# A hybrid encoder layer on one core: operand stores on another queue, and a norm's last blocks moved among the next products

## The chip, the core and the metric

The kernel runs on one core of one Trainium2 chip. TensorE (PE) multiplies, with its weight loads (PEld) beside it; VectorE (DVE), ScalarE (ACT) and GpSimd (POOL) compute; SyncE (SP), ACT and POOL issue DMAs, each from a queue that is worked off in order. The time is device microseconds of one execution; the median of the runs counts.

## What is computed

One encoder layer over 2048 frames of width 1024, in float32. Cut to what matters here:

```
mix = concat([y_pool, y_ssm]) @ w_out
h = layer_norm(alpha * h + mix, g1, b1)
f = (silu(h @ w1) * (h @ w3)) @ w2        # w1, w3: 1024 x 2816, w2: 2816 x 1024
r = alpha * h + f
h = layer_norm(r + sigmoid(r @ w_gate) * (p @ w_ple), g2, b2)
```

with alpha = 2 ** 0.25. Everything up to `mix` (input projection, pooling, state space, GLU) and the last line are untouched by the change.

## The kernel before

**Products.** Each float32 operand is split into a high and a low part (`split`, L100 to 102: a cast on ACT, a subtraction on VectorE), and each product is three matmuls (`mm3`, L122 to 125). In the gated unit the 2048 frames stand as two halves h of 1024, and each multiplication of 2 x 2 blocks is done with seven products in place of eight. `pieces7` (L826) forms the seven operands: its `put` (L834) splits one into a tile `xo` (tag `xb`, two buffers in `xbp`, L1249) and stores it, 512 KB, to DRAM (L837): `Gv` for the pieces of g = silu(.) * (.), 154 stores, `Xv` for pieces of h, 28, `Wv` for pieces of the gate's weights, 28. All 210 go out on POOL's queue. They come back as `gv` (L996, POOL), `xv` and `gw`.

**Stages around the change.** `out_proj` adds the mix to `pre`; `out_ln(h, q)` (L712) normalises 512 frames: statistics of four blocks on VectorE, a power on POOL (L739), the normalisation on ACT (L718), 32 transposes on TensorE into `zb` (L722), copies into `ze` (L724) and stores to DRAM `Hd` on ACT's queue (L725). `load_h` (L858) loads 128 columns of `Hd` on POOL's queue, multiplies by g1 and adds b1 (L861, VectorE), and stores the result to `Hn` (L862, 16 stores of 512 KB on POOL's queue). `xprep0` and `xprep0_rest` make the pieces `xv` of half 0 from it, `xprep1` those of half 1, which `put` stores. `w13(h)` then runs 11 pairs of columns with 2 x 7 products of twelve matmuls each into banks `fb`; ACT and VectorE form g from the banks (L943 to L970), and `pieces7` of g runs beside the next pair's products. `w2_half(h)` multiplies by w2: `gv` pieces against weight pieces into banks `f`; the first result for a tile `HR` is an ACT copy (L1025), later ones are added by VectorE (L1026); once a tile is full, `hl` is loaded from `Hn` on SP's queue (L1015) and VectorE adds ALPHA * hl (L1016). The HR tiles share the memory of the g tiles (`slp`, tag `sl`), so the third one waits until the last g has been read by the sixth piece's split, put(5). Weights `wq` come on SP's queue (L774, three buffers), five products ahead (LEAD); sums of them (`ws`) and the pieces `wv` are made by ACT and VectorE, the sums in tiles `x` (five buffers), of which `pre` takes four.

**Order.** A scheduler orders each engine's instructions from a simulated timeline; the order of the program's text and the rates given to `drive` (steps of the second generator for each step of the first) shape it. Around the change the program's text is:

```
for _ in range(2):
    more()                                  # weights, one product each
drive(out_ln(1, 1), xprep0_rest(), 0.5)
for _ in range(2, LEAD):
    more()
drive(w13(0), xprep1(), 0.5)
drive(w2_half(0), None, 0)
```

Of the kernel before, what the change touches and what calls it, by code (L numbers as in the profile page):

```python
# [12 lines left out]
F32 = mybir.dt.float32  # L13
# [27 lines left out]
def trunk_kernel(  # L41
# [120 lines left out]
    Td = drp.tile([128, NG, 128], F32, name="Td")  # L162
    Rd = drp.tile([NC, 16, 2, 240], F32, name="Rd")
    Gd = drp.tile([128, NG, 128], F32, name="Gd")
    Hn = drp.tile([2, 8, 128, 2, 512], F32, name="Hn")
    Xv = drp.tile([7, 4, 128, 1024], F32, name="Xv")
    Gv = drp.tile([2, NF // 2, 7, 128, 1024], F32, name="Gv")
    Wv = drp.tile([7, 4, 128, 1024], F32, name="Wv")
# [540 lines left out]
            for t in range(4):  # L709
                V.scalar_tensor_tensor(pre[t][:, ns], pre[t][:, ns], ALPHA, acc[t], MUL, ADD)  # L710

    def out_ln(h, q):  # L712
        pre = blk[h, q][3]
        for t in range(4):
            mv, rstd = ln_stats([pre[t][:, 0:512], pre[t][:, 512:1024]])
            nb = sm.tile([128, 1], F32, tag="nb", name="nb")
            V.scalar_tensor_tensor(nb, mv[:, 0:1], -1.0, rstd, MUL, MUL)
            A.activation(pre[t], pre[t], AF.Identity, bias=nb, scale=rstd)  # L718
            for m2 in range(2):
                b = tbank([128, 4, 128], "zb")  # L720
                for m in range(4):
                    PE.transpose(b[:, m], pre[t][:, 512 * m2 + 128 * m:512 * m2 + 128 * m + 128], ident)  # L722
                e = evp.tile([128, 4, 128], F32, tag="ev", name="ze")
                A.copy(e, b)  # L724
                A.dma_start(Hd[512 * m2:512 * m2 + 512, h, 4 * q + t].rearrange("(m p) j -> p m j", p=128), e)  # L725
            yield
# [86 lines left out]
    def all_weights():  # L813
        for h in range(2):
            for pi in range(NF // 2):
                for w in (w1, w3):
                    yield from weights7(w[2 * pi], w[2 * pi + 1], 1)
            for gi, pairs in W2:
                np_ = len(pairs)
                for mu in range(np_):  # L820
                    yield from weights7(w2[4 * gi + mu], w2[4 * gi + np_ + mu], np_, sums_b if gi else sums_x)
        for n in range(len(PAIRS)):
            yield from rows7(n)
# [5 lines left out]
    def pieces7(b11, b12, b21, b22, dst):  # L829

        tt = xp.tile([128, 2, 512], F32, tag="x", name="tt")
        t1, t2 = tt[:, 0], tt[:, 1]

        def put(i, src):  # L834
            v = operand(xbp, "xb", "xo")
            split(v[:, 0], v[:, 1], src)
            G.dma_start(dst[i], v.bitcast(F32).rearrange("p a n -> p (a n)"))  # L837

        put(0, b11)
        yield  # L840
# [12 lines left out]
        put(5, b22)
        yield
        put(6, t2)
        yield

    def load_h(h, k, pool, tag):  # L858
        t = pool.tile([128, 2, 512], F32, tag=tag, name="hl")
        G.dma_start(t, Hd[128 * k:128 * k + 128, h].rearrange("p (q t) j -> p q (t j)", q=2))  # L860
        V.tensor_scalar(t, t, g1[:, k:k + 1], b1[:, k:k + 1], MUL, ADD)  # L861
        G.dma_start(Hn[h, k], t)  # L862
        return t

    X = [[[None] * 4 for _ in range(7)] for _ in range(2)]
# [114 lines left out]
    def w2_half(h):  # L980
# [19 lines left out]
        for gi, pairs in W2:  # L1000
# [3 lines left out]
            for mu in range(np_):  # L1004
                if gi == 0:
                    t = slp.tile([128, 2, 2, 512], F32, tag="sl", name="HR")
                    hr[2 * mu], hr[2 * mu + 4] = t[:, 0], t[:, 1]
                    for m in (2 * mu + 1, 2 * mu + 5):
                        hr[m] = operand32("HR", mu)
                else:  # L1010
                    um = per_units[gi] + mu
                    if um < 8:
                        hl = xp.tile([128, 2, 512], F32, tag="x", name="hl")
                        with tc.issue_after(latest[0].ins):
                            SP.dma_start(hl, Hn[h, um])  # L1015
                        V.scalar_tensor_tensor(hr[um], hl, ALPHA, hr[um], MUL, ADD)  # L1016
                done_w = []
                for m0 in range(0, per, 2):
                    ms = [per * mu + m0, per * mu + m0 + 1]
# [229 lines left out]
    xbp = mid_pools.enter_context(tc.tile_pool(name="xbp", bufs=2, reuse_waits="tile"))  # L1249
    wqp = mid_pools.enter_context(tc.tile_pool(name="wqp", bufs=3, reuse_waits="tile"))  # L1250
    stream[0] = all_weights()
    for _ in range(2):
        more()
    drive(out_ln(1, 1), xprep0_rest(), 0.5)
    for _ in range(2, LEAD):
        more()
    drive(w13(0), xprep1(), 0.5)
    drive(w2_half(0), None, 0)
    xload1(latest[0])
    drive(w13(1), wprep(), 0.5)  # L1260
# [79 lines left out]
```

## Time and profile before

| | |
|---|---|
| timed runs | 2088.03, 2088.08, 2091.39 us, median 2088.08 |
| the profiled execution | 2085.38 us, of which the span is 2083.6 |
| mean granted clock of TensorE | 0.986 |
| busy: TensorE, VectorE, ACT, POOL | 2008.1, 1611.5, 876.8, 337.0 us |
| mean DMA rate | 218 GB/s |

The rows are of the profiled execution. PEclk is the clock granted to TensorE, as a share of full speed. In a timeline row the bracket holds the idle time of that engine before the instruction and what ended it, as inferred from semaphores; a matmul's length includes what overlaps the next one.

### The profile page before, as it was taken

To read this page: it belongs to the slowest core of one execution; us is meant where nothing else is said; L and a number is where in the kernel's file an instruction comes from. 1 tells how busy PE (TensorE), PEld (TensorE's weight loads), DVE (VectorE), ACT (ScalarE), POOL (GpSimd) and SP (SyncE) were. 2 spreads that over 40 slices of the span, in tenths; PEclk is the share of its full clock that TensorE was granted. 3 is DMA by queue.
4 is the path that set the end of the run, shared out by engine and by line. 5 is a ranking of instruction groups with operands and counts; after the bars stand their busy time and mean duration, and the time that the engine had idled before them with its cause. 6 is when DMAs were issued, how large, how long until landed. Compare 5 with 4: busy or idle time off the path is not lost.

```text
span 2083.6 us, 25684 instructions
## 1 busy us (share of the span) xinstructions
PE 2008.1 (96%) x8968; PEld 1626.0 (78%) x8968; DVE 1611.5 (77%) x2886; ACT 876.8 (42%) x1515; POOL 337.0 (16%) x595
## 2 busy tenths in 40 slices
PE   8999899999899999999899999999999799999996
PEld 6877778787688878888688888888888688878885
DVE  7599699658678887676698878887776588878885
ACT  3543546645544554444322245555444322233342
POOL 2002101211112111103122111111012221211111
PEclk9999999999999999999999999999999999999998
DMA  7636757657646754439777775665346986782221
GB/s 248 221 109 227 263 181 233 232 192 263 211 188 247 257 209 159 165 122 373 302 290 295 289 245 222 236 229 197 127 151 211 390 314 255 283 288 91 92 71 46
DMA packets 161041, 454.45 MB, mean 218 GB/s; under 512 B 15424, under 2 KB 51616, under 8 KB 160912
## 3 DMA queue, kind: packets, MB, share of 16 engines
q0 software_dynamic: 73632, 265.10, 34.1%
q1 hardware_dynamic: 53296, 156.26, 21.6%
q10 hardware_dynamic: 33984, 31.46, 4.4%
q8 instruction: 70, 1.15, 0.2%
q14 instruction: 59, 0.48, 0.1%
HBM read 291.83 MB, written 163.02 MB: 218 GB/s over the span
## 4 chain that ended last, share of the span: by engine, by line
PE 54%; issue 20%; DMA 12%; DVE 7%; POOL 4%; ACT 3%; POOLq 0%; SPq 0%; ACTq 0%; DVEq 0%
PE f L123 6%; PE f L124 6%; PE f L125 6%; PE fb L123 6%; PE fb L125 5%; PE fb L124 5%; PE ab L123 2%; PE ab L124 2%; PE ab L125 2%; DMA Gv<-xo 2%; PE ib L125 2%; PE ib L123 2%; PE ib L124 2%; POOL Gv L837 2%; DMA hl<-Hd 2%
## 5 line engine op out<-in xcount | busy, mean ns | idle before, releaser
L123 PE MATMUL fb<-xv,wv 128*128 128x512 f32 x1232 | 482.9, 396 | 6.6 <-ACT u L967 4.8
L124 PE MATMUL fb<-xv,wv 128*128 128x512 f32 x1232 | 485.6, 394 | 0.0
L125 PE MATMUL fb<-xv,wv 128*128 128x512 f32 x1232 | 479.9, 395 | 0.2 <-DVE wv L102 0.2
L101 ACT CAST wv<-ws 128x512 fp32r<-128x512 f32 x296 | 183.3, 620 | 384.1 <-PE f L125 170.5
L123 PEld LDWEIGHTS fb<-xv,wv 128*128 128x128 f32 x1232 | 232.4, 189 | 62.0 <-ACT u L967 7.1
L125 PEld LDWEIGHTS fb<-xv,wv 128*128 128x128 f32 x1232 | 232.1, 188 | 54.1 <-DVE wv L102 0.7
L124 PEld LDWEIGHTS fb<-xv,wv 128*128 128x128 f32 x1232 | 232.4, 189 | 53.5
L123 PE MATMUL f<-gv,wv 128*128 128x512 f32 x616 | 242.7, 397 | 19.6 <-ACT HR L1025 17.1
L102 DVE TENSOR_TENSOR wv<-ws,wv 128x512 fp32r<-128x512 f32 x296 | 202.9, 686 | 68.3 <-ACT wv L101 67.9
L124 PE MATMUL f<-gv,wv 128*128 128x512 f32 x616 | 243.9, 396 | 0.0
L1026 DVE TENSOR_TENSOR HR<-HR,f 128x512 f32<-128x512 f32 x304 | 201.1, 682 | 45.7 <-PE f L125 42.2
L125 PE MATMUL f<-gv,wv 128*128 128x512 f32 x616 | 234.3, 396 | 0.0
L837 POOL DMA_DIRECT2D Gv<-xo x154 | 82.2, 534 | 562.7 <-DVE xo L102 549.2
L101 ACT CAST wv<-wq 128x512 fp32r<-128x512 f32 x198 | 122.7, 621 | 96.7 <-PE f L125 73.0
L123 PEld LDWEIGHTS f<-gv,wv 128*128 128x128 f32 x616 | 116.9, 190 | 49.1 <-ACT HR L1025 18.4
L102 DVE TENSOR_TENSOR wv<-wq,wv 128x512 fp32r<-128x512 f32 x198 | 135.4, 685 | 20.2 <-ACT wv L101 19.7
L125 PEld LDWEIGHTS f<-gv,wv 128*128 128x128 f32 x616 | 116.8, 190 | 26.7
L124 PEld LDWEIGHTS f<-gv,wv 128*128 128x128 f32 x616 | 116.8, 190 | 26.3
L101 ACT CAST xo<-tt 128x512 fp32r<-128x512 f32 x120 | 74.6, 621 | 120.1 <-DMA Gv<-xo 49.2
L996 POOL DMA_DIRECT2D gv<-Gv x154 | 81.6, 530 | 228.1 <-PE f L125 181.0
L102 DVE TENSOR_TENSOR xo<-tt,xo 128x512 fp32r<-128x512 f32 x120 | 82.3, 686 | 40.1 <-ACT xo L101 39.5
L123 PE MATMUL ob<-wh,mx 128*128 128x512 f32 x256 | 102.3, 409 | 7.4 <-ACT sg L681 7.4
(317 smaller groups left out, 3551.8 us busy)
## 6 DMA issues: line engine op xcount, KB each, us to landing
Gv<-xo POOLq DMA_DIRECT2D x154, 512.0 KB, 3.2
gv<-Gv POOLq DMA_DIRECT2D x154, 512.0 KB, 7.6
wq<-in_w_dram SPq DMA_DIRECT2D x132, 512.0 KB, 4.3
wr<-in_w_out_dram SPq DMA_DIRECT2D x32, 512.0 KB, 4.7
Xv<-xo POOLq DMA_DIRECT2D x28, 512.0 KB, 3.8
xv<-Xv POOLq DMA_DIRECT2D x28, 512.0 KB, 5.8
Wv<-xo POOLq DMA_DIRECT2D x28, 512.0 KB, 3.3
gw<-Wv POOLq DMA_DIRECT2D x28, 512.0 KB, 5.8
```

What stands on the lines that cost most here:

```text
L101: A.copy(hi, src)
L102: V.tensor_tensor(lo, src, hi.bitcast(F32), SUB)
L123: PE.matmul(ps, ah, bh, start=first, stop=False, **kw)
L124: PE.matmul(ps, ah, bl, start=False, stop=False, **kw)
L125: PE.matmul(ps, al, bh, start=False, stop=last, **kw)
L837: G.dma_start(dst[i], v.bitcast(F32).rearrange("p a n -> p (a n)"))
L996: G.dma_start(v.bitcast(F32).rearrange("p a n -> p (a n)"), Gv[h, pi, i])
L1026: return V.tensor_tensor(o, o, bank, ADD)
```

## The change

1. `put` stores on SP's queue (all 210 stores).
2. `Hn` and its 16 stores are gone. `w2_half` loads `hl` from `Hd`, the normalised values before g1 and b1; VectorE multiplies by alpha * g1, a scalar per partition, in place of alpha, and alpha * b1 comes in as the bias of an ACT activation that takes the place of the copy into HR. Both vectors are made once, by two small VectorE instructions.
3. `out_ln(1, 1)` no longer runs before `w13(0)` but beside it, chained ahead of `xprep1()`, at one step for two products; its `ze` tiles come from another pool, and the sums of the first w1 weights lie in an `xb` tile, since `pre` still holds four of the `x` tiles.

```
@@ -141,6 +141,9 @@
     glub = column("glub", glu_b, 4)
     g1 = column("g1", ln1_g, 8)
     b1 = column("b1", ln1_b, 8)
+    gb1a = cst.tile([128, 2, 8], F32, name="gb1a")
+    V.tensor_scalar(gb1a[:, 0], g1, ALPHA, None, MUL)
+    V.tensor_scalar(gb1a[:, 1], b1, ALPHA, None, MUL)
     poolw = cta.tile([128, 4, 128], F32, name="poolw")
     G.dma_start(poolw, pool_w[0].rearrange("g c d -> c g d"))
 
@@ -162,7 +165,6 @@
     Td = drp.tile([128, NG, 128], F32, name="Td")
     Rd = drp.tile([NC, 16, 2, 240], F32, name="Rd")
     Gd = drp.tile([128, NG, 128], F32, name="Gd")
-    Hn = drp.tile([2, 8, 128, 2, 512], F32, name="Hn")
     Xv = drp.tile([7, 4, 128, 1024], F32, name="Xv")
     Gv = drp.tile([2, NF // 2, 7, 128, 1024], F32, name="Gv")
     Wv = drp.tile([7, 4, 128, 1024], F32, name="Wv")
@@ -709,7 +711,7 @@
             for t in range(4):
                 V.scalar_tensor_tensor(pre[t][:, ns], pre[t][:, ns], ALPHA, acc[t], MUL, ADD)
 
-    def out_ln(h, q):
+    def out_ln(h, q, room=None):
         pre = blk[h, q][3]
         for t in range(4):
             mv, rstd = ln_stats([pre[t][:, 0:512], pre[t][:, 512:1024]])
@@ -720,7 +722,7 @@
                 b = tbank([128, 4, 128], "zb")
                 for m in range(4):
                     PE.transpose(b[:, m], pre[t][:, 512 * m2 + 128 * m:512 * m2 + 128 * m + 128], ident)
-                e = evp.tile([128, 4, 128], F32, tag="ev", name="ze")
+                e = evp.tile([128, 4, 128], F32, tag="ev", name="ze") if room is None else room([128, 4, 128], "ze")
                 A.copy(e, b)
                 A.dma_start(Hd[512 * m2:512 * m2 + 512, h, 4 * q + t].rearrange("(m p) j -> p m j", p=128), e)
             yield
@@ -814,7 +816,7 @@
         for h in range(2):
             for pi in range(NF // 2):
                 for w in (w1, w3):
-                    yield from weights7(w[2 * pi], w[2 * pi + 1], 1)
+                    yield from weights7(w[2 * pi], w[2 * pi + 1], 1, sums_b if h + pi == 0 and w is w1 else sums_x)
             for gi, pairs in W2:
                 np_ = len(pairs)
                 for mu in range(np_):
@@ -834,7 +836,7 @@
         def put(i, src):
             v = operand(xbp, "xb", "xo")
             split(v[:, 0], v[:, 1], src)
-            G.dma_start(dst[i], v.bitcast(F32).rearrange("p a n -> p (a n)"))
+            SP.dma_start(dst[i], v.bitcast(F32).rearrange("p a n -> p (a n)"))
 
         put(0, b11)
         yield
@@ -859,7 +861,6 @@
         t = pool.tile([128, 2, 512], F32, tag=tag, name="hl")
         G.dma_start(t, Hd[128 * k:128 * k + 128, h].rearrange("p (q t) j -> p q (t j)", q=2))
         V.tensor_scalar(t, t, g1[:, k:k + 1], b1[:, k:k + 1], MUL, ADD)
-        G.dma_start(Hn[h, k], t)
         return t
 
     X = [[[None] * 4 for _ in range(7)] for _ in range(2)]
@@ -1012,8 +1013,8 @@
                     if um < 8:
                         hl = xp.tile([128, 2, 512], F32, tag="x", name="hl")
                         with tc.issue_after(latest[0].ins):
-                            SP.dma_start(hl, Hn[h, um])
-                        V.scalar_tensor_tensor(hr[um], hl, ALPHA, hr[um], MUL, ADD)
+                            SP.dma_start(hl, Hd[128 * um:128 * um + 128, h].rearrange("p (q t) j -> p q (t j)", q=2))
+                        V.scalar_tensor_tensor(hr[um], hl, gb1a[:, 0, um:um + 1], hr[um], MUL, ADD)
                 done_w = []
                 for m0 in range(0, per, 2):
                     ms = [per * mu + m0, per * mu + m0 + 1]
@@ -1022,7 +1023,7 @@
                     def add(m, q, bank, new):
                         o = hr[m][:, q]
                         if new and gi == 0:
-                            return A.copy(o, bank)
+                            return A.activation(o, bank, AF.Identity, bias=gb1a[:, 1, m:m + 1])
                         return V.tensor_tensor(o, o, bank, ADD)
 
                     for i in range(7):
@@ -1249,12 +1250,11 @@
     xbp = mid_pools.enter_context(tc.tile_pool(name="xbp", bufs=2, reuse_waits="tile"))
     wqp = mid_pools.enter_context(tc.tile_pool(name="wqp", bufs=3, reuse_waits="tile"))
     stream[0] = all_weights()
-    for _ in range(2):
+    for _ in xprep0_rest():
         more()
-    drive(out_ln(1, 1), xprep0_rest(), 0.5)
     for _ in range(2, LEAD):
         more()
-    drive(w13(0), xprep1(), 0.5)
+    drive(w13(0), chain(out_ln(1, 1, sbig), xprep1()), 0.5)
     drive(w2_half(0), None, 0)
     xload1(latest[0])
     drive(w13(1), wprep(), 0.5)
```

**TensorE, the start of w13(0).** `zb` are the transposes of `out_ln(1, 1)`, `fb` the products' banks. Before:

```order
L123 MATMUL fb_5032<-xv_5011,wv_5022 128x512
L124 MATMUL fb_5032<-xv_5011,wv_5022 128x512
L125 MATMUL fb_5032<-xv_5011,wv_5022 128x512
L722 MATMUL zb_4896<-ident_102,pre_4619 128x128 x4
L722 MATMUL zb_4904<-ident_102,pre_4619 128x128 x4
L722 MATMUL zb_4922<-ident_102,pre_4621 128x128 x4
L722 MATMUL zb_4930<-ident_102,pre_4621 128x128 x4
L123 MATMUL fb_5174<-xv_4440,wv_5077 128x512
L124 MATMUL fb_5174<-xv_4440,wv_5077 128x512
L722 MATMUL zb_4960<-ident_102,pre_4623 128x128 x4
L722 MATMUL zb_4968<-ident_102,pre_4623 128x128 x4
L722 MATMUL zb_4986<-ident_102,pre_4625 128x128 x4
```

After, the first of the four groups:

```order
L125 MATMUL fb_4922<-xv_4738,wv_4926 128x512
L123 MATMUL fb_4922<-xv_4854,wv_4926 128x512
L124 MATMUL fb_4922<-xv_4854,wv_4926 128x512
L724 MATMUL zb_4969<-ident_102,pre_4615 128x128 x4
L724 MATMUL zb_4977<-ident_102,pre_4615 128x128 x4
L125 MATMUL fb_4922<-xv_4854,wv_4926 128x512
L125 MATMUL fb_5130<-xv_4443,wv_5005 128x512
L123 MATMUL fb_4920<-xv_4379,wv_4942 128x512
```

Before, 28 of the 32 transposes (seven rows of four) stand nearly together behind the first products; after, the first eight stand 49 rows of the listing later, inside a product, and the other three groups 23, 22 and 20 rows behind one another.

**ACT, the switch from w13(0) to w2_half(0).** `xo` are the splits of the last g's pieces, `HR` the copies of the first w2 results. Before, from a little ahead of the third piece (`xo_8523`):

```order
L1025 COPY HR_8628<-f2_8633 128x512
L101 CAST wv_8657<-wq_8502 128x512
L101 CAST xo_8523<-tt_8470 128x512
L101 CAST wv_8678<-wq_8674 128x512
L1025 COPY HR_8629<-f2_8635 128x512
L1025 COPY HR_8628<-f2_8633 128x512
L101 CAST xo_8548<-tt_8470 128x512
L1025 COPY HR_8629<-f2_8633 128x512
L101 CAST xo_8575<-tt_8470 128x512
L101 CAST xo_8601<-g_8120 128x512
L1025 COPY HR_8627<-f2_8630 128x512
```

After, around the second and third piece (`xo_8482`, `xo_8509`), and then the fourth to the sixth:

```order
L101 CAST xo_8482<-g_8106 128x512
L1026 ACTIVATE HR_8430<-f2_8433,gb1a_120 128x512
L101 CAST xo_8509<-tt_8456 128x512
L1026 ACTIVATE HR_8431<-f2_8436,gb1a_120 128x512
L101 CAST wv_8513<-wq_8486 128x512
```

```order
L1026 ACTIVATE HR_8615<-f2_8621,gb1a_120 128x512
L101 CAST xo_8534<-tt_8456 128x512
L1026 ACTIVATE HR_8614<-f2_8619,gb1a_120 128x512
L101 CAST xo_8561<-tt_8456 128x512
L1026 ACTIVATE HR_8615<-f2_8619,gb1a_120 128x512
L101 CAST xo_8587<-g_8106 128x512
L1026 ACTIVATE HR_8613<-f2_8616,gb1a_120 128x512
```

The third piece has moved twelve instructions up, from between the HR results to directly behind the second piece; the fourth to the sixth stand about where they stood, and the result for the third HR tile (`HR_8627` before, `HR_8613` after) is behind the sixth as before.

**POOL before and SP after, the same switch.** The stores of the third to the seventh piece. Before, on POOL:

```order
L996 DMA gv_8824<-Gv_141 128x1024
L996 DMA gv_8826<-Gv_141 128x1024
L996 DMA gv_8866<-Gv_141 128x1024
L996 DMA gv_8868<-Gv_141 128x1024
L837 DMA Gv_141<-xo_8523 128x1024
L996 DMA gv_8909<-Gv_141 128x1024
L996 DMA gv_8911<-Gv_141 128x1024
L837 DMA Gv_141<-xo_8548 128x1024
L837 DMA Gv_141<-xo_8575 128x1024
L837 DMA Gv_141<-xo_8601 128x1024
L837 DMA Gv_141<-xo_8623 128x1024
```

After, on SP:

```order
L839 DMA Gv_143<-xo_8482 128x1024
L839 DMA Gv_143<-xo_8509 128x1024
L776 DMA wq_8662<-in_w2_dram 128x1024
L776 DMA wq_8814<-in_w2_dram 128x1024
L1016 DMA hl_8767<-Hd_138 128x1024
L839 DMA Gv_143<-xo_8534 128x1024
L839 DMA Gv_143<-xo_8561 128x1024
L839 DMA Gv_143<-xo_8587 128x1024
L839 DMA Gv_143<-xo_8609 128x1024
L776 DMA wq_8816<-in_w2_dram 128x1024
```

The stores have left the row of gv loads on POOL and stand between weight loads (`wq`) and the reload of h (`hl`) on SP.

## Rows read from the trace of the kernel before

**Rows 1.** The page's first part: busy time, share of the span, instructions of each engine

```profile
PE 2008.1 (96%) x8968; PEld 1626.0 (78%) x8968; DVE 1611.5 (77%) x2886; ACT 876.8 (42%) x1515; POOL 337.0 (16%) x595
```

**Rows 2.** TensorE's waits over the whole run: us in total, times, longest

```profile
PE f L123 <- ACT HR L1025: 17.1, 3, 9.9
...
PE fb L125 <- DVE wv L102: 0.2, 1, 0.2
```

**Rows 3.** Windows: length, busy PE, PEld, DVE, ACT, POOL (count), PEclk, DMA share, GB/s

```profile
515.00:525.00 10.00, 9.76 (x43) 7.65 (x42) 10.00 (x18) 2.48 (x4) 0.00 (x0) 1.00 0.00 0
525.00:530.00 5.00, 3.21 (x18) 2.25 (x16) 2.75 (x15) 3.45 (x4) 2.42 (x4) 1.00 0.00 0
530.00:540.00 10.00, 7.70 (x31) 6.38 (x32) 5.93 (x10) 7.46 (x14) 0.00 (x0) 0.66 0.79 246
540.00:545.00 5.00, 3.76 (x19) 2.86 (x17) 1.38 (x2) 3.50 (x5) 0.89 (x2) 1.00 0.56 166
545.00:555.00 10.00, 6.39 (x22) 4.89 (x21) 5.76 (x9) 4.47 (x8) 1.83 (x4) 0.83 0.83 281
1000.00:1010.00 10.00, 4.49 (x17) 2.69 (x16) 4.37 (x6) 1.20 (x2) 0.54 (x1) 0.97 0.81 331
1010.00:1020.00 10.00, 7.58 (x25) 6.12 (x26) 6.84 (x11) 5.53 (x10) 4.25 (x8) 0.69 0.67 238
1650.00:1665.00 15.00, 5.71 (x24) 4.04 (x22) 5.59 (x8) 1.82 (x3) 2.13 (x4) 0.88 0.93 377
1665.00:1675.00 10.00, 8.61 (x27) 6.86 (x28) 7.87 (x13) 4.98 (x9) 4.25 (x8) 0.67 0.68 245
```

**Rows 4.** Timeline, switch of half 1: start, length, engine, operation [idle before, releaser]

```profile
1649.06 0.62 ACT L101 CAST xo<-tt 128x512 fp32r<-128x512 f32 x1
...
1654.34 0.54 POOL L837 DMA_DIRECT2D Gv<-xo  x1 [0.91 <-DMA gv<-Gv]
...
1664.38 0.62 ACT L101 CAST xo<-g 128x512 fp32r<-128x512 f32 x1 [3.10 <-DMA Gv<-xo]
...
1666.39 0.79 PE L123 MATMUL f<-gv,wv 128*128 128x512 f32 x1 [9.90 <-ACT HR L1025]
```

**Rows 5.** Timeline, the same steps of half 0

```profile
997.48 0.62 ACT L101 CAST xo<-tt 128x512 fp32r<-128x512 f32 x1
...
999.39 0.54 POOL L837 DMA_DIRECT2D Gv<-xo  x1 [1.81 <-DMA gv<-Gv]
...
1010.41 0.62 ACT L101 CAST xo<-g 128x512 fp32r<-128x512 f32 x1 [3.10 <-DMA Gv<-xo]
...
1012.42 0.79 PE L123 MATMUL f<-gv,wv 128*128 128x512 f32 x1 [6.48 <-ACT HR L1025]
```

**Rows 6.** DMA issues of 990 to 1000: count, KB each, median us to landing

```profile
Gv<-xo POOLq DMA_DIRECT2D x2, 512.0 KB, 11.5
wq<-in_w_dram SPq DMA_DIRECT2D x1, 512.0 KB, 8.1
hl<-Hn SPq DMA_DIRECT2D x1, 512.0 KB, 10.2
```

**Rows 7.** DMA issues of 1640 to 1650

```profile
Gv<-xo POOLq DMA_DIRECT2D x1, 512.0 KB, 12.5
```

**Rows 8.** The page's groups of instructions: POOL's store issues | busy, mean | idle before

```profile
L837 POOL DMA_DIRECT2D Gv<-xo x154 | 82.2, 534 | 562.7 <-DVE xo L102 549.2
```

**Rows 9.** Timeline behind the norm's last transposes: TensorE, ACT, TensorE

```profile
540.45 0.60 PE L722 MATMUL zb<-ident,pre 128*128 128x128 f32 x4
...
547.78 0.62 ACT L101 CAST xo<-hl 128x512 fp32r<-128x512 f32 x1 [3.60 <-DVE hl L861]
...
548.93 0.79 PE L123 MATMUL fb<-xv,wv 128*128 128x512 f32 x1 [3.61 <-ACT u L967]
```

**Rows 10.** Groups by shape on ACT: copies into HR, sigmoids with a bias

```profile
L1025 ACT COPY HR<-f 128x512 f32<-128x512 f32 x32 | 18.6, 588 | 35.6 <-PE f L125 34.0 <-DVE xo L102 1.5
...
L681 ACT ACTIVATE sg<-gb,glub 128x512 f32<-128x512 f32 x16 | 10.4, 683 | 7.0 <-PE gb L125 5.1 <-DVE mx L102 1.9
```

More of the change, by code (lines that the diff above doesn't have):

```diff
@@ L143, in trunk_kernel @@
     b1 = column("b1", ln1_b, 8)
+    gb1a = cst.tile([128, 2, 8], F32, name="gb1a")
+    V.tensor_scalar(gb1a[:, 0], g1, ALPHA, None, MUL)
+    V.tensor_scalar(gb1a[:, 1], b1, ALPHA, None, MUL)
     poolw = cta.tile([128, 4, 128], F32, name="poolw")
@@ L164, in trunk_kernel @@
     Gd = drp.tile([128, NG, 128], F32, name="Gd")
-    Hn = drp.tile([2, 8, 128, 2, 512], F32, name="Hn")
     Xv = drp.tile([7, 4, 128, 1024], F32, name="Xv")
@@ L710, in out_proj, with out_ln @@
                 V.scalar_tensor_tensor(pre[t][:, ns], pre[t][:, ns], ALPHA, acc[t], MUL, ADD)
-    def out_ln(h, q):
+    def out_ln(h, q, room=None):
         pre = blk[h, q][3]
@@ L722, in out_ln @@
                     PE.transpose(b[:, m], pre[t][:, 512 * m2 + 128 * m:512 * m2 + 128 * m + 128], ident)
-                e = evp.tile([128, 4, 128], F32, tag="ev", name="ze")
+                e = evp.tile([128, 4, 128], F32, tag="ev", name="ze") if room is None else room([128, 4, 128], "ze")
                 A.copy(e, b)
@@ L816, in all_weights @@
                 for w in (w1, w3):
-                    yield from weights7(w[2 * pi], w[2 * pi + 1], 1)
+                    yield from weights7(w[2 * pi], w[2 * pi + 1], 1, sums_b if h + pi == 0 and w is w1 else sums_x)
             for gi, pairs in W2:
@@ L836, in put @@
             split(v[:, 0], v[:, 1], src)
-            G.dma_start(dst[i], v.bitcast(F32).rearrange("p a n -> p (a n)"))
+            SP.dma_start(dst[i], v.bitcast(F32).rearrange("p a n -> p (a n)"))
         put(0, b11)
@@ L861, in load_h @@
         V.tensor_scalar(t, t, g1[:, k:k + 1], b1[:, k:k + 1], MUL, ADD)
-        G.dma_start(Hn[h, k], t)
         return t
@@ L1014, in w2_half @@
                         with tc.issue_after(latest[0].ins):
-                            SP.dma_start(hl, Hn[h, um])
-                        V.scalar_tensor_tensor(hr[um], hl, ALPHA, hr[um], MUL, ADD)
+                            SP.dma_start(hl, Hd[128 * um:128 * um + 128, h].rearrange("p (q t) j -> p q (t j)", q=2))
+                        V.scalar_tensor_tensor(hr[um], hl, gb1a[:, 0, um:um + 1], hr[um], MUL, ADD)
                 done_w = []
@@ L1024, in add @@
                         if new and gi == 0:
-                            return A.copy(o, bank)
+                            return A.activation(o, bank, AF.Identity, bias=gb1a[:, 1, m:m + 1])
                         return V.tensor_tensor(o, o, bank, ADD)
@@ L1251, in trunk_kernel @@
     stream[0] = all_weights()
-    for _ in range(2):
+    for _ in xprep0_rest():
         more()
-    drive(out_ln(1, 1), xprep0_rest(), 0.5)
     for _ in range(2, LEAD):
         more()
-    drive(w13(0), xprep1(), 0.5)
+    drive(w13(0), chain(out_ln(1, 1, sbig), xprep1()), 0.5)
     drive(w2_half(0), None, 0)
```

## The prediction

> **What bounds the kernel now.** First the busy times: TensorE works 2008.1 us of the 2083.6 us span [rows 1], the next engine, VectorE, 1611.5. No other engine can be the bound over the whole, so the change can win only what TensorE stands still (75.5 us) and what it runs under a lowered clock. Second, what TensorE waited for: the largest entry is the gated unit's second matrix waiting for the ACT copy into an HR tile, 17.1 us in three waits, 9.9 in one of them; it hardly ever waits for weight pieces (0.2 us on VectorE's half of a split) [rows 2]. Third, the stretches in which this stands [rows 3]; the reader should subtract PE busy from the length and then look at PEclk:
> - 515 to 555, the last norm of the first half of the kernel (out_ln(1,1)) and the gated unit's start: idle 0.24 + 1.79 + 2.30 + 1.24 + 3.61 = 9.2 us. The clock was granted at 0.66 over 7.70 busy us and at 0.83 over 6.39, against 1.00 before: 7.70 x 0.34 + 6.39 x 0.17 = 3.7 us. Together 12.9 us.
> - 1000 to 1020, the switch from w1/w3 to w2 for half 0: idle 5.5 + 2.4 = 7.9 us, clock 7.58 x 0.31 = 2.3 us.
> - 1650 to 1675, the same switch for half 1: idle 9.3 + 1.4 = 10.7 us, clock 8.61 x 0.33 = 2.8 us.
> These three places hold 37 us. The rest of the idle time (the start, the ssm stages, the last norm at the end) is untouched.
>
> Why the switches stall is in the timelines [rows 4, 5]. The last operand tile is split by ACT and VectorE into one of two xb buffers and stored to DRAM; a buffer is free only when its store has landed. In half 1 ACT cast the fourth piece at 1649.06, VectorE needs 0.7 us more, but the store went out at 1654.34, as POOL's queue is in order and a gv load ahead of it was waiting (the row's releaser is a DMA). The sixth piece's cast, at 1664.38, waited for this store [3.10 <-DMA Gv<-xo]. HR's third tile takes the memory of the g that this cast reads, so ACT's copy into it came after, and TensorE went on at 1666.39, 2.0 us behind the cast. In half 0 the same steps are 997.48, 999.39, 1010.41 and 1012.42.
>
> **The change part by part.**
>
> *Stores on SyncE's queue.* Two gains are possible: the store no longer stands behind gv loads, and it may land sooner. In these stretches the DMA engines are full (93% over 1650 to 1665 [rows 3]). In 990 to 1000 a store on POOL's queue took 11.5 us to land, a load on SP's queue 8.1 and 10.2, all of 512 KB [rows 6]; in 1640 to 1650 the store took 12.5 [rows 7]. No store on SP's queue stands there, so its time is bounded by 8.1 below and by the 12.5 of a POOL store above; I take 8.1 to 10.2, since the new order puts the store directly behind such a load on the same queue. The store can go out when VectorE's half is done, 1.4 us after the cast's start: 998.9 in half 0 (0.5 us sooner than now), 1650.5 in half 1 (3.9 sooner). It lands at 1007.0 to 1009.1 and at 1658.6 to 1660.7; 2.0 us later TensorE goes on, at 1009.0 to 1011.1 instead of 1012.42 and at 1660.6 to 1662.7 instead of 1666.39. That saves 1.3 to 3.4 us and 3.7 to 5.8 us; I take 2.5 and 5. The third piece is cast twelve ACT instructions earlier in half 0, so the fifth, which shares its buffer, shouldn't be late next. A shorter stall also costs less clock: of 2.3 and 2.8 us I count 1 and 1.5 back, from nothing to all as ends. Half 0: 3.5 us (1 to 6); half 1: 6.5 us (3 to 9).
>
> The Trainium skill, page "DMA: Bandwidth & Descriptors", section "Issuing engines are not separate DMA queues", speaks against the second gain: DMAs of all issuing engines end up on the same 16 engines and interleave, and a second issuing engine saves only issue time. By that rule the store would land no sooner, which is the first rival below. The same page's "Queues, rings and completion order" says that each engine goes round between the queue rows it has work for, packet by packet, which fits the 8.1 against 11.5 us of the two queues here: a queue with few transfers would get its share sooner. The trace bears the latter out for loads; no run here shows it for stores.
>
> What SP's queue pays: 210 stores (154 + 28 + 28) enter a queue that carries the weight loads. On POOL the 154 stores of g waited 549.2 us at the head of their queue for VectorE's half of the split [rows 8], 3.6 us each. On SP a load behind such a store is held as long. I take nothing for it: in the new order each store and load on SP waits for a VectorE instruction that comes later in VectorE's own order than that of the one before it, so no load is held by a store whose piece is younger than the buffer that the load needs; and loads run five products ahead. The dearer end is the slower rival.
>
> *The last norm in pieces.* The statistics of all four blocks, the four normalisations and the 32 transposes stood in one go between the first products; TensorE reached the transposes and waited, and the clock fell. Now they come in four groups of eight, each between full products, with the first group later. The transposes themselves cost the same. Of the 12.9 us, 3.6 idle and about 1.1 of clock come from a step behind the norm: ACT's cast of the freshly loaded hl, which waited for the load from Hd (3.60) and held the copy that TensorE wanted [rows 9]. It ran 7.3 us after the last transposes (540.45 to 547.78). In the new order 38 matmuls stand between the last transposes and the end of the product whose copy is queued behind this cast, at 2008.1 / 8968 = 0.22 us each 8.5 us, so it fits, with little over. VectorE is the danger: it was busy 10.00 of 10 us from 515 to 525 while TensorE was fed just in time [rows 3]; the norm's statistics leave that stretch, which loosens it. I count 12 of the 12.9 us back, with 7 and 13 as ends.
>
> *h not stored a second time.* 16 stores, 8 MB, and their issues on POOL go; the reload reads Hd in pieces of the same size, and VectorE's multiply takes a per-partition scalar in place of a constant. No critical wait names Hn, so nothing. ACT's 32 copies into HR become activations with a bias: a plain copy took 588 ns, a sigmoid of the same shape with a bias 683 [rows 10], so up to 0.1 us each, 3 us over the kernel on an engine that is 42% busy [rows 1]; one or two stand on the path of a switch: 0.2 us, left out. The two tiny scalings at the start and the other buffer for the first weight sums: nothing.
>
> Sum: 12 + 3.5 + 6.5 = 22 us. The profiled execution took 2085.4 us (1.8 outside the span), the timed runs' median is 2088.1; from these, 2063.4 and 2066.1. I put 2065.
>
> **The rivals.**
> 1. *Stores land no sooner.* With 11.5 and 12.5 us on SP too, half 0 gains nothing (998.9 + 11.5 = 1010.4) and half 1 lands at 1663.0, 1.4 us sooner. Then 12 + 1.4 = 13.4: about 2075. For it: the DMA engines are full there. Against: the loads on SP's queue.
> 2. *The boundary's wait moves.* The first products come sooner, and VectorE's pieces for them don't; or the cast of hl is late again (the fit above is 1 us wide). Then only the switches gain: 10 us, about 2078. For it: VectorE's 10.00 of 10 us; against: TensorE's wait on it there was only 0.24 us.
> 3. *Slower: weight loads held on SP.* A load has five products of 12 matmuls, 13.4 us, less its landing of 8.1 when the engines are full: 5.3 us to spare. Two stores in a row that wait 3.6 us each, 7.2, would overrun it by 1.9 us; once in each of the 22 units (11 pairs, two halves) that is 42 us, about 2107. It decides from a hold of over 5.3 us; then TensorE's waits on wv, 0.2 us now, would be the largest entry. Against it: the order of releases on SP, and that in most of w1/w3 the engines aren't full.
> 4. *Nothing moves on the whole.* The switches wait for another step of the last operand (its VectorE pieces, a gv load) and rival 2 holds: about 2086.
>
> **How the numbers follow.** Chances: forecast 0.55, rival 1 0.18, rival 2 0.12, rival 3 0.08, rival 4 0.07. The forecast's own range is 2057 to 2077 by its ends (13 + 6 + 9 = 28 saved from 2085.4, 7 + 1 + 3 = 11 from 2088.1). The range of 8 in 10 is 2054 to 2080: it takes in rivals 1 and 2 and a little for a switch stall that goes wholly, and leaves out 3, 4 and the tails. A measurement of this kernel tells 0.2% (4.2 us) from no change: faster by more 0.84 (forecast, rivals 1 and 2, less 0.01), within 0.08, slower 0.08.
>
> **What would show it.** Right: the wait of f for ACT's HR falls from 17.1 to some 9 us; PEclk stays 1.00 through the first products, and the idle of that stretch is under 2 us; the transposes stand in four groups without waits before them; Gv<-xo on SP's queue lands in 8 to 10 us where the engines are full. Rival 1: it lands in over 11 us there. Rival 2: fb waits for VectorE's or ACT's pieces or for u around 520 to 550. Rival 3: waits on wv, spread over the units of w1 and w3. What would make the sum wrong without any of these: the static order of the three engines shifts elsewhere, above all in the gate stage at the end, which I count at nothing.

## The result

The changed kernel takes 2059.4 us (median of 6 runs, 2055.6 to 2065.0) against 2089.7 us for the kernel before; the ratio is 0.9858, 95% interval 0.9833 to 0.9883, some 30 us less. That lies inside the range and 6 us below the forecast of 2065. Its profiled execution took 2065.0 us with a span of 2063.0.

TensorE's waits in the profile of the changed kernel, columns as in [rows 2] (lines 1026, 968, 997 and so on are the old ones moved down by one to three):

```profile
PE f L123 <- ACT HR L1026: 7.7, 3, 4.0
...
PE f L123 <- ACT wv L101: 2.1, 1, 2.1
PE fb L123 <- ACT u L968: 1.9, 1, 1.9
PE f L125 <- DVE wv L102: 1.3, 1, 1.3
PE zb L724 <- ACT ze L726: 1.1, 1, 1.1
```

The row for zb in the kernel before was:

```profile
PE zb L722 <- ACT ze L724: 5.0, 2, 2.8
```

The wait for HR fell from 17.1 to 7.7 us, that of zb for ze from 5.0 to 1.1. Weight pieces for f are a new entry. Below are, in the changed kernel, the same windows as in [rows 3] for the boundary (515 to 555, the norm and the start of w13(0)), and the two switches where they now stand:

```profile
515.00:525.00 10.00, 10.00 (x44) 8.12 (x43) 10.00 (x19) 4.53 (x8) 0.00 (x0) 1.00 0.15 52
525.00:530.00 5.00, 5.00 (x23) 4.04 (x22) 3.76 (x13) 3.42 (x6) 2.30 (x4) 1.00 0.31 105
530.00:540.00 10.00, 10.00 (x49) 8.25 (x48) 4.70 (x12) 8.62 (x13) 0.73 (x1) 1.00 0.10 28
540.00:545.00 5.00, 5.00 (x28) 4.15 (x27) 3.44 (x6) 3.00 (x7) 0.00 (x0) 1.00 0.89 270
545.00:555.00 10.00, 10.00 (x53) 8.35 (x52) 5.62 (x10) 5.48 (x10) 0.00 (x0) 1.00 0.52 153
980.00:990.00 10.00, 7.35 (x30) 5.04 (x28) 4.22 (x7) 2.49 (x4) 0.00 (x0) 1.00 1.02 413
990.00:1000.00 10.00, 7.08 (x24) 5.68 (x25) 7.92 (x13) 5.26 (x9) 3.17 (x6) 0.83 0.65 233
1635.00:1650.00 15.00, 10.10 (x41) 7.02 (x39) 7.71 (x11) 4.39 (x7) 3.17 (x6) 1.00 1.00 395
1650.00:1660.00 10.00, 7.71 (x21) 5.84 (x22) 8.58 (x15) 2.90 (x6) 0.00 (x0) 0.66 0.98 398
```

The boundary is full at full clock: nothing is left of the 12.9 us. The switches still stall, for less.

The switch of half 1 in the changed kernel, to be read against [rows 4]: the fourth piece's cast, the sixth piece's cast and TensorE behind HR; the last two rows are new.

```profile
1631.59 0.61 ACT L101 CAST xo<-tt 128x512 fp32r<-128x512 f32 x1
...
1641.09 0.62 ACT L101 CAST xo<-g 128x512 fp32r<-128x512 f32 x1
...
1643.21 0.50 PE L123 MATMUL f<-gv,wv 128*128 128x512 f32 x1 [2.94 <-ACT HR L1026]
...
1648.88 0.69 DVE L793 TENSOR_TENSOR ws<-wq 128x512 f32<-128x512 f32 x1 [3.85 <-DMA Gv<-xo]
...
1651.00 0.50 PE L123 MATMUL f<-gv,wv 128*128 128x512 f32 x1 [2.10 <-ACT wv L101]
```

From the fourth piece's cast to the sixth's it is 9.5 us now and was 15.3; the sixth no longer waits for a store. But 5 us later VectorE waits 3.85 us for a store, and TensorE for the pieces made from that sum.

The same steps of half 0, to be read against [rows 5], with VectorE's half of the sixth piece as a row of its own:

```profile
979.06 0.61 ACT L101 CAST xo<-tt 128x512 fp32r<-128x512 f32 x1
...
988.75 0.62 ACT L101 CAST xo<-g 128x512 fp32r<-128x512 f32 x1 [1.55 <-DMA Gv<-xo]
...
991.47 0.68 DVE L102 TENSOR_TENSOR xo<-g,xo 128x512 fp32r<-128x512 f32 x1
...
992.92 0.50 PE L123 MATMUL f<-gv,wv 128*128 128x512 f32 x1 [4.02 <-ACT HR L1026]
```

Here too the sixth cast comes sooner, 9.7 us behind the fourth where it was 12.9. But VectorE's half follows only 2.7 us later, as VectorE first adds two results to HR and multiplies hl between them. TensorE goes on 4.2 us behind the cast, where it was 2.0.

How much each stretch lost, in each profile, is worked out from windows of 5 us as in [rows 3]: idle time of TensorE plus busy time times (1 - PEclk), summed over the stretch. The variants are those of the next section.

| idle + clock, us | 0-480 | 480-515 | 515-600 | 960-1030 (switch 0) | 1600-1690 (switch 1) |
|---|---|---|---|---|---|
| before | 21.9 + 5.7 | 2.3 + 0.0 | 9.2 + 3.8 | 8.9 + 2.0 | 10.7 + 2.6 |
| before, second profile | 16.1 + 4.1 | 3.7 + 2.5 | 9.5 + 4.3 | 7.0 + 2.4 | 10.0 + 2.3 |
| stores_sp_only | 22.1 + 4.6 | 3.8 + 2.8 | 9.8 + 3.8 | 5.3 + 1.3 | 7.5 + 2.6 |
| norm_ahead | 23.4 + 3.8 | 1.5 + 0.0 | 8.3 + 4.7 | 5.6 + 2.7 | 3.7 + 1.2 |
| norm_ahead_room | 22.6 + 7.8 | 0.8 + 0.0 | 3.2 + 0.0 | 5.6 + 1.2 | 6.6 + 1.7 |
| hn_kept | 23.2 + 4.0 | 5.4 + 3.0 | 1.4 + 0.0 | 5.3 + 2.3 | 6.7 + 4.3 |
| stores_pool | 22.4 + 5.4 | 0.0 + 0.0 | 0.0 + 0.0 | 8.6 + 2.2 | 10.3 + 2.1 |
| swap | 24.7 + 8.9 | 1.6 + 0.0 | 0.0 + 0.0 | 8.2 + 2.5 | 8.2 + 4.1 |
| changed | 22.7 + 4.4 | 1.1 + 0.0 | 0.0 + 0.0 | 6.6 + 1.2 | 7.2 + 2.8 |
| changed, second profile | 23.9 + 5.7 | 0.3 + 0.0 | 0.0 + 0.0 | 5.6 + 3.0 | 5.0 + 1.2 |
| ze_room | 25.3 + 2.6 | 0.0 + 0.0 | 0.7 + 0.0 | 5.6 + 1.6 | 6.5 + 2.9 |
| sums_x1 | 18.7 + 2.9 | 0.4 + 0.0 | 0.0 + 0.0 | 5.7 + 0.0 | 5.6 + 1.5 |
| sums_x | 20.8 + 4.3 | 0.0 + 0.0 | 0.0 + 0.0 | 5.7 + 1.6 | 6.0 + 1.6 |
| ze_room_sums | 21.0 + 3.7 | 0.0 + 0.0 | 1.5 + 0.0 | 4.8 + 5.6 | 5.9 + 2.9 |

The first column is work that no variant touches on purpose (kernels with `Hn` send its first stores there, from 442 us on); it loses 20 to 34 us from profile to profile. Single executions of one kernel differ by some 10 us, and only the stretches can be compared between single profiles. The two profiled executions of the kernel before (2085.4 and 2078.4 us) lie below its median, the two of the changed kernel (2065.0 and 2061.8) above its own: taken in order, whole profiles show a gain of 20.4 and 16.6 us, and not the 30 of the medians.

### The profile page after: what moved, and what is told of

It is laid out like the page before. It is cut to its first block, busy times and chain, and to the rows that moved or that the text cites. A ratio compares the mean times of both kernels' runs of the same rounds, so it can differ in the third digit from the quotient of the medians.

```text
span 2063.0 us, 25651 instructions
## 1 busy us (share of the span) xinstructions
PE 2001.9 (97%) x8968; PEld 1624.1 (79%) x8968; DVE 1612.9 (78%) x2888; ACT 881.2 (43%) x1515; POOL 216.9 (11%) x369
## 4 chain that ended last, share of the span: by engine, by line
PE 80%; DMA 9%; DVE 7%; issue 2%; ACT 2%; POOL 0%; SPq 0%; POOLq 0%; ACTq 0%; DVEq 0%
PE fb L125 12%; PE fb L123 12%; PE fb L124 12%; PE f L125 6%; PE f L123 6%; PE f L124 6%; PE ab L123 2%; PE ab L124 2%; PE ab L125 2%; PE ib L125 2%; PE ib L123 2%; PE ib L124 2%; PE ob L123 2%; PE ob L124 2%; DMA Gv<-xo 2%
## 5 line engine op out<-in xcount | busy, mean ns | idle before, releaser
L123 PE MATMUL ib<-xT,wh 128*128 128x512 f32 x256 | 101.6, 406 | 6.1 <-ACT xT L101 6.0
```

Of the source, the lines that this page charges most:

```text
L123: PE.matmul(ps, ah, bh, start=first, stop=False, **kw)
```

## The experiments

Ratios are to the kernel before, with 95% intervals. Medians of the kernel before, run beside them, were 2089.7 to 2090.5 us.

**The norm ahead again.** The changed kernel with the old order of the text:

```
-    for _ in xprep0_rest():
+    for _ in range(2):
         more()
+    drive(out_ln(1, 1), xprep0_rest(), 0.5)
     ...
-    drive(w13(0), chain(out_ln(1, 1, sbig), xprep1()), 0.5)
+    drive(w13(0), xprep1(), 0.5)
```

> The changed kernel with the last first norm again in one go ahead of the gated unit's first products; stores and reload as in the change. Theory (the norm's place alone made the boundary's gain): the stretch from 515 to 555 us has again some 9 us of idle TensorE and a granted clock of 0.66 to 0.85 in parts of it, and the time is that of the changed kernel plus 10 to 13 us, about 2070 to 2073. Rival (the boundary got better because the stores left POOL's queue, or h is stored once less): the boundary keeps its full TensorE and the time stays within 4 us of 2059.

Measured: 2081.1 us, ratio 0.9964 (0.9943 to 0.9986), some 21 us over the changed kernel and 8 over the end of what was expected. TensorE's windows of it:

```profile
525.00:535.00 10.00, 6.22 (x33) 4.51 (x32) 5.57 (x19) 7.24 (x9) 2.73 (x4) 0.95 0.25 79
535.00:545.00 10.00, 7.51 (x24) 5.47 (x24) 0.69 (x1) 5.43 (x8) 1.10 (x2) 0.50 0.65 201
545.00:555.00 10.00, 8.01 (x31) 5.90 (x31) 7.05 (x11) 4.89 (x9) 0.00 (x0) 0.87 0.62 200
```

The idle time and the low clock are back, 8.3 + 4.7 = 13.0 us by the table, so the norm's move made this gain and the stores did not. The profiled execution (2074.1 us, the fastest of its seven) was 9 us over that of the changed kernel (2065.0, the slowest of its six); the median is 21 over. Where the timed executions lose the further 8 us can't be seen in a profile, and stays open.

**Room or place.** The new order gave the norm two things: a later place in the text, and six buffers for ze in place of three. This variant takes back the place alone; against the variant before it, the edit is:

```
-    drive(out_ln(1, 1), xprep0_rest(), 0.5)
+    drive(out_ln(1, 1, sbig), xprep0_rest(), 0.5)
```

> The changed kernel with the last first norm ahead of the gated unit in the program's text, as in norm_ahead, but its ze tiles still from the larger pool (six buffers in place of three shared with other copies). TensorE's order then has the 32 transposes in four groups, at the same rows of the listing as in the changed kernel, without the text being moved. Theory A (the gain at the boundary is the room for ze, which lets the scheduler spread the transposes): the boundary is full as in the changed kernel, and the time 2057 to 2064. Theory B (the place in the text counts, as VectorE's statistics and ACT's normalisations still come first): idle time of 5 us or more and a lowered clock between 515 and 560, time 2068 to 2083.

Measured: 2069.2 us, ratio 0.9893 (0.9867 to 0.9919). By time this is theory B, 2068 to 2083; by the trace of 515 to 555 it is theory A. TensorE's waits of this variant:

```profile
PE fb L123 <- ACT u L968: 3.7, 4, 1.5
...
PE fb L125 <- DVE wv L102: 2.6, 3, 1.8
```

515 to 555 is full at full clock, as in the changed kernel; what is lost stands behind it (3.2 us between 555 and 600, 1.6 between 600 and 960), most of it waiting for VectorE's pieces and for u, 1.8 us in one case. So the room let the scheduler spread the transposes, 12 us by the medians (2081.1 to 2069.2), and the place gave another 10 (to 2059.4); of that the profile shows 5. That the place gains by keeping VectorE in step fits the waits, but is not shown by itself.

**Stores on POOL's queue again.** The changed kernel with the store in `put` issued by POOL:

```
-            SP.dma_start(dst[i], v.bitcast(F32)...)
+            G.dma_start(dst[i], v.bitcast(F32)...)
```

> The changed kernel with the 210 operand stores on POOL's queue again. Theory (the store queue made the gain at the two switches): the stores of the last g take 11 us and more to land there again, TensorE's wait of f for ACT's HR goes from 7.7 us back towards 17, and the time rises by 5 to 9 us, to 2064 to 2068; the boundary stays full. Rival (the switches gained because ACT's order puts the third piece earlier, which this kernel has in half 0 or not by its own order, or because less traffic is left): wait of f for HR under 10 us, time within 3 us of 2059.

Measured: 2065.4 us, ratio 0.9891 (0.9871 to 0.9911), 6 us over the changed kernel. TensorE's wait, then the DMA issues of 975 to 990 in this variant:

```profile
PE f L123 <- ACT HR L1026: 17.3, 3, 9.5
```

```profile
gv<-Gv POOLq DMA_DIRECT2D x4, 512.0 KB, 13.0
wq<-in_w_dram SPq DMA_DIRECT2D x1, 512.0 KB, 8.1
hl<-Hd SPq DMA_DIRECT2D x1, 512.0 KB, 10.2
Gv<-xo POOLq DMA_DIRECT2D x1, 512.0 KB, 11.6
```

The stores of the fourth piece, in half 0 and in half 1 of this variant:

```profile
981.94 0.54 POOL L839 DMA_DIRECT2D Gv<-xo  x1 [2.18 <-DVE xo L102]
...
1635.95 0.54 POOL L839 DMA_DIRECT2D Gv<-xo  x1 [1.57 <-DMA gv<-Gv]
```

The whole wait is back (17.1 before). In half 0 the store went out 0.3 us behind VectorE's half, so there it was the landing time of 11.6 us, and not its place in POOL's queue, that made TensorE wait. In half 1 it went out 3.7 us behind VectorE's half, held by a gv load, so there the place counted too. The switches lose 10.8 and 12.4 us, as before.

**Stores on SP's queue, nothing else.** The kernel before with only that line changed:

> The kernel before with the operand stores on SP's queue, and nothing else changed. Theory (the store queue is worth what the two switches gain): wait of f for HR about 7 to 9 us in place of 17.1, stores landing in 7 to 9 us where the DMA engines are full, the boundary as before with its 13 us, time 2080 to 2085. Rival (this part pays only together with the norm's move, or weight loads are held on SP): 2087 or more, with waits on wv.

Measured: 2080.7 us, ratio 0.9956 (0.9941 to 0.9972): 9 us gained alone, as the theory has it. The wait for HR is 7.5 us, the boundary keeps its 13.6 us.

**Two queues swapped.** The gv loads on SP among the weight loads, the stores alone on POOL:

```
-                    G.dma_start(v.bitcast(F32)..., Gv[h, pi, i])
+                    SP.dma_start(v.bitcast(F32)..., Gv[h, pi, i])
     ...
-            SP.dma_start(dst[i], v.bitcast(F32)...)
+            G.dma_start(dst[i], v.bitcast(F32)...)
```

> The changed kernel with two queues swapped: the gv loads on SP's queue among the weight loads, the operand stores on POOL's, which then carries no gv loads. Theory (full DMA engines share their time between queues, so that the queue with few transfers lands sooner, whichever engine issues): the last stores land on POOL's queue in 6 to 9 us in place of 11 to 12, and weight loads and hl on SP behind the gv loads in over 10. Rival (stores land sooner on SP because its issue path is quicker as such): they take 11 to 12 us on POOL here too. Time: the held weight loads cost something at each switch, 2062 to 2085 by the first, 2075 to 2095 by the second.

Measured: 2063.7 us, ratio 0.9875 (0.9846 to 0.9905). The DMA issues of 970 to 985 in this variant, and of 980 to 990 in the changed kernel:

```profile
gv<-Gv SPq DMA_DIRECT2D x9, 512.0 KB, 11.2
wq<-in_w_dram SPq DMA_DIRECT2D x2, 512.0 KB, 11.3
Gv<-xo POOLq DMA_DIRECT2D x1, 512.0 KB, 6.9
```

```profile
Gv<-xo SPq DMA_DIRECT2D x2, 512.0 KB, 8.4
```

The theory holds for the landing: here the transfer on the queue with little else on it lands soon, whichever engine issues. On POOL the store landed in 6.9 us, and the weight loads, now behind the gv loads on SP, in 11.3 in place of 8.1. The Trainium skill, page "DMA: Bandwidth & Descriptors", says in "Issuing engines are not separate DMA queues" that another issuing engine saves only issue time; with full DMA engines that was not so here, 6.9 and 8.4 against 11.6 us. What the same page of the Trainium skill says in "Queues, rings and completion order", that the engines go round between queues, agrees with the 6.9 and 11.2 us of this variant.

For the switches the quick store was not enough. They lose 10.7 and 12.3 us in this profile, as much as with the stores among the gv loads (10.8 and 12.4), and TensorE still waits 13.0 us for HR:

```profile
PE f L123 <- ACT HR L1026: 13.0, 3, 6.7
```

```profile
997.22 1.28 DVE L1017 SCALAR_TENSOR_TENSOR HR<-hl,gb1a,HR 128x1024 f32<-128x1024 f32 x1 [1.98 <-DMA hl<-Hd]
...
1651.26 1.28 DVE L1017 SCALAR_TENSOR_TENSOR HR<-hl,gb1a,HR 128x1024 f32<-128x1024 f32 x1 [3.23 <-DMA hl<-Hd]
```

The load of hl now stands behind the gv loads, and VectorE, whose half of the sixth piece comes behind this multiplication, waits for it. The full queue has moved the wait to another transfer.

**h stored a second time.** The changed kernel with `Hn`, its 16 stores, the reload from it and the plain copies:

```
+        G.dma_start(Hn[h, k], t)
...
-                            SP.dma_start(hl, Hd[128 * um:128 * um + 128, h]...)
-                        V.scalar_tensor_tensor(hr[um], hl, gb1a[:, 0, um:um + 1], hr[um], MUL, ADD)
+                            SP.dma_start(hl, Hn[h, um])
+                        V.scalar_tensor_tensor(hr[um], hl, ALPHA, hr[um], MUL, ADD)
...
-                            return A.activation(o, bank, AF.Identity, bias=gb1a[:, 1, m:m + 1])
+                            return A.copy(o, bank)
```

> The changed kernel, but normalised h is stored a second time (16 stores on POOL's queue), reloaded from there, multiplied by a constant, and HR gets plain copies, as in the kernel before. Theory (this part is worth nothing): within 2 us of the changed kernel, 2057 to 2062, no new wait of TensorE. Rival (8 MB less traffic and shorter POOL queue are worth something at the pieces of h): 3 to 6 us more, with waits of fb between 540 and 760. Other rival (the biased copy costs on the switch's path): 1 to 2 us less.

Measured: 2062.9 us, ratio 0.9883 (0.9861 to 0.9905). That is 2 to 3 us over the changed kernel and 1 over the theory's range, but by time alone it can't be told from the changed kernel. Of the waits of fb that the first rival had between 540 and 760 there is one, 1.4 us. The profile shows a place where it is not nothing, and not the one expected: 480 to 515, while the norm before the last runs beside out_proj. The window, the wait of TensorE and the DMA issues of 475 to 500, first of this variant, then (window and issues) of the changed kernel:

```profile
480.00:515.00 35.00, 29.54 (x129) 23.82 (x128) 23.28 (x34) 12.29 (x19) 2.66 (x5) 0.90 0.79 273
```

```profile
PE zb L725 <- ACT ze L727: 5.5, 1, 5.5
```

```profile
Hn<-hl POOLq DMA_DIRECT2D x3, 512.0 KB, 7.9
hl<-Hd POOLq DMA_DIRECT2D x3, 512.0 KB, 8.8
Hd<-ze ACTq DMA_DIRECT2D x5, 256.0 KB, 11.4
```

```profile
480.00:515.00 35.00, 33.85 (x156) 27.23 (x155) 32.74 (x49) 18.75 (x31) 1.05 (x2) 1.00 0.71 237
```

```profile
Hd<-ze ACTq DMA_DIRECT2D x8, 256.0 KB, 3.5
hl<-Hd POOLq DMA_DIRECT2D x4, 512.0 KB, 6.9
```

The three ze buffers come free when their stores have landed. With the stores to Hn on their way these took 8.4 and 7.8 us (two profiles of before), 6.9 (stores_sp_only) and 11.4 (hn_kept); without them, in eight profiles with the ze buffers left as they are there, 3.5 to 7.2. The table's second column follows: 2.3, 6.2, 6.6 and 8.4 us, mean 5.9, against 0 to 1.6, and a clock of 1.00 in all eight. The landing times of the two groups overlap a little (6.9 and 7.2), the losses don't. ACT's ze copies waited for Hd's stores between 475 and 515 in both groups, 9.0 to 11.3 us with the stores to Hn and 4.7 to 6.7 without; in this variant, then in the changed kernel:

```profile
ACT ze L727 <- DMA Hd<-ze: 11.3, 3, 8.2
```

```profile
ACT ze L726 <- DMA Hd<-ze: 6.0, 2, 4.2
```

A kernel with the stores to Hn and more ze buffers, which would show the link by itself, was not run.

**More room for that norm.** The changed kernel with the six buffers for the norm before the last, too:

```
-    ... out_proj(1, 1, out_ln(1, 0))
+    ... out_proj(1, 1, out_ln(1, 0, sbig))
```

> The changed kernel with the larger pool for ze in the norm before the last, too (out_ln(1,0), beside out_proj). Around 494 us TensorE waited there for a ze copy, and ACT for a store Hd<-ze to land, between nothing and 5.5 us in the profiles so far (before 2.3, changed 1.2, the variant with h kept 5.5 with a clock of 0.70 behind it). Theory (the three ze buffers wait for stores of uneven landing time): no wait there, 490 to 510 full, and the spread of the single times smaller, 2054 to 2060. Rival (the wait moves into the start of the gated unit): 2058 to 2064 with a new wait of fb.

Measured: 2058.1 us, ratio 0.9841 (0.9820 to 0.9861). No ze copy waits for a store any more, and 480 to 515 is full. Its single times spread as much as before (2052.2 to 2061.8), and the median is not distinguishable from the changed kernel's: with the stores to Hn gone there was only 1 us left to gain.

**The sums out of the operands' buffers.** The new wait at the switch of half 1: sums of w2's second group of weights no longer in tiles xb.

```
-  ... sums_b if gi else sums_x)
+  ... sums_b if gi > 1 else sums_x)
```

> The changed kernel with one thing else: the sums of the weights of w2's second group lie in tiles x in place of tiles xb. In the changed kernel, at the switch of half 1, VectorE's first sum for that group waited 3.85 us with a store Gv<-xo named as the releaser, and TensorE then 2.10 + 1.30 us for weight pieces with the clock at 0.60 to 0.71 behind it. Theory (the sums share the two xb buffers with the operands and wait until the last stores have landed): this wait is gone, and the time falls by 3 to 6 us, to 2053 to 2056. Rival (VectorE really waited for the weight load, queued on SP behind the stores): TensorE waits as long as before for wv, time unchanged at 2059.

Measured: 2055.2 us, ratio 0.9844 (0.9823 to 0.9866). TensorE's waits of it:

```profile
PE f L123 <- DVE HR L1027: 8.8, 5, 3.1
...
PE f L123 <- ACT HR L1026: 0.8, 1, 0.8
```

VectorE's sums wait for no store of a piece and TensorE for no weight piece in w2, so the shared buffers were the cause of the new wait, and not the weight load. But 8.8 us now go to HR from VectorE, and the switch of half 1 loses 7.1 us, inside what the two profiles of the changed kernel lost (10.0 and 6.2). With the sums of all groups moved:

> The changed kernel with the weight sums of all of w2's later groups in tiles x, none in xb. Theory (what counts is that the sums don't wait for the last operand stores, which only the second group's sums can): as the variant with the second group alone, 2052 to 2058 us, no wait of TensorE for wv at the switches. Rival (tiles x are short, as hl and HR lie in them too): new waits for HR or hl in w2, 2060 or more.

Measured: 2061.2 us, ratio 0.9865 (0.9840 to 0.9889), the rival's time, with 9.0 us waited for HR from VectorE. And with ze_room and sums_x1 together:

> ze_room and sums_x1 in one kernel. Theory (the two waits are apart, 490 to 510 and at the switch of half 1): both gone, 2050 to 2056. Rival (each only moves a wait): 2057 to 2062.

Measured: 2062.4 us, ratio 0.9864 (0.9840 to 0.9888), not the theory's 2050 to 2056. So the wait was found, and taking it away moved it: none of the three is shown to beat the changed kernel, whose interval each of theirs overlaps.

**Both kernels once more.** The changed kernel beside its variants:

> The changed kernel itself, once more, beside the others of this call on the same chip, since its single executions spread over some 10 us. Every theory: 2059 us, ratio to the kernel before 0.983 to 0.988; its profile shows the boundary full, the wait of f for ACT's HR 7 to 9 us, and at the switch of half 1 the weight pieces 3 to 4 us late.

Measured: 2060.6 us, ratio 0.9861 (0.9837 to 0.9884). The boundary is full, the wait for HR 7.7 us; at the switch of half 1 VectorE's first sum again waited for a store, 2.83 us, but TensorE only 1.4 us for weight pieces, less than expected. The kernel before, for a second profile:

> The kernel before once more, for a second profile of it: its timed runs have a median some 4 us above the one profiled execution. Theory (the wait for ze copies around 490 to 500 and the boundary's clock differ from execution to execution): idle and slow clock between 480 and 560 add up to 15 to 22 us in this profile, against 15.6 in the first. Rival (they differ elsewhere, in the first 450 us or at the switches): 480 to 560 as before within 2 us, other stretches more.

Measured: one execution of 2078.4 us. 480 to 600 lost 20.0 us against 15.3 in the first profile, which the expectation had at 15.6 (the theory), but the first 480 us lost 20.2 against 27.6 (the rival): both vary.

## Why the prediction was right, step by step

- **What bounds the kernel: right.** The gain came out of TensorE's idle time and clock; the places named lost it.
- **The norm in pieces: mechanism right, worth more than counted.** 12 of 12.9 us were counted, and in the trace all 12.9 came back. The cast of hl that fits by 1 us did fit: from 545 to 555 nothing waits. What was not seen is that the room for ze does half of it. By medians the step is worth 20 to 22 us (norm_ahead to the changed kernel: 2081.1 to 2059.4 and 2060.6 us), above the 13 that the prediction had as its upper end; some 8 of them stand in no profile, and their cause stays open.
- **Stores on SP's queue: mechanism right, sum a little high, half 1 mis-sized.** The landing of 8.1 to 10.2 us was measured at 8.4 in half 0. Half 0: 3.5 us counted; the two profiles before lost 10.9 and 9.4 there and the changed ones 7.8 and 8.6, 2 us. TensorE's wait behind HR fell by the 2.5 us that were counted (6.48 to 4.02), but "2.0 us later TensorE goes on" did not hold: it was 4.2, behind VectorE's sums into HR and its multiplication of hl. The wait is 4.02 us in both profiles of the changed kernel, in norm_ahead and in norm_ahead_room alike, so it is this chain on VectorE, and no longer the landing, that bounds half 0; rival 4 had named VectorE's pieces. Half 1: 6.5 counted; 13.3 and 12.3 before, 10.0 and 6.2 after, 4.7. TensorE's wait behind HR did fall by 7.0 us (9.90 to 2.94), 2 more than counted. What was overlooked stands in the sentence on what is late next: the order was searched for the fifth piece, which shares the third's buffer, and not for the weight sums, which use the same two buffers. They took back 3.4 us in the first profile, with a clock of 0.66 behind it, and 1.4 us in the second. By medians the store queue is worth 9 us alone and 5 to 6 in the changed kernel, against 10 counted.
- **h not stored again: not shown to be nothing.** It was put at nothing because no critical wait names Hn. The waits named Hd, whose stores land later when those to Hn are on their way: about 5 us between 480 and 515 by the profiles, but only 2 to 3 by medians, which can't be told from nothing. The 2.3 us idle there in the first profile were counted among the untouched rest. The copies with a bias took 688 ns against 588 [rows 10], the 0.1 us that was expected; TensorE's wait in half 0 is 4.02 us with them and 3.86 with plain copies (stores_sp_only, hn_kept).
- **The sum: too low, and nearer than its terms.** 22 us were counted and 29 to 30 measured. By medians the stores alone give 9 us and the norm alone 20 to 22, together the whole difference; 10 and 12 had been counted. So the norm's term was some 9 us too low and the stores' term 1 to 5 too high. That these partly cancelled, and the forecast came within 6 us, is in part luck. By the table's means the terms are 13 (boundary), 2 and 4.7 (switches) and 5 (480 to 515), 25 together, but whole profiles differ by only 20.4 and 16.6 us, partly as the first 480 us lost more in the changed kernel's profiles (27.1 and 29.6 us) than in those of before (27.6 and 20.2). What of the medians' 30 us stands in no stretch stays open.
- **The rivals.** Stores that land no sooner: refuted by 8.4 us and by the swap. The boundary's wait moving: seen only in norm_ahead_room, where the text's place was taken back. Nothing moving on the whole: refuted, but its first half, the switch waiting for VectorE's pieces, is what half 0 shows. Slower, weight loads held on SP: stores do stand at the head of SP's queue, as the second row below of the changed kernel shows, 516.8 us over 209 of them or 2.5 us each. But the loads' own wait for a buffer fell by as much, from 1095.5 to 541.4 us, and no product waited for a load.

```profile
SPq L776 <- DVE wv L102: 541.4, 121, 19.1
SPq L839 <- DVE xo L102: 516.8, 209, 17.5
```

  In the kernel before, the loads' wait for a buffer was:

```profile
SPq L774 <- DVE wv L102: 1095.5, 122, 17.5
```

## What to carry to other kernels

Where the DMA engines are full, put the one transfer that somebody waits for on a queue that carries little else; which engine issues it mattered less here. Then look at what is left on the full queue: with the two queues swapped the store was quick and the load of hl late. When a resource's users are searched for what comes late next, list every tile of that pool, and every instruction that an engine does ahead of the freed step, not only those of the chain at hand. A transfer that no wait names can still cost, through the transfers that it delays: look at the landing times beside it before writing nothing.

## What was not expected of the hardware

At the switch of half 0 a 512 KB store landed in 8.4 us on SP's queue and in 11.6 on POOL's among the gv loads (median 13.0); with the queues swapped it landed in 6.9 on POOL's, and the gv and weight loads, now together on SP's, in 11.2 and 11.3. The 256 KB stores of ze took 3.5 us at the least and 11.4 with three 512 KB stores beside them. And the first 480 us, nearly the same work in every variant, lost between 20 and 34 us of TensorE from one execution to the next, and a single profile stands up to 11 us off its kernel's median (2078.4 against 2089.7).
